# Three layer norms of a decoder layer: the turns of the last columns behind the second half's sums, vectors and residual columns loaded later

## The chip, the cores and the metric

The kernel runs on one core of a Trainium2 chip. TensorE (PE) multiplies and transposes into PSUM; VectorE (DVE) and ScalarE (ACT) work on SBUF and PSUM; SyncE (SP) issues nearly all DMAs; GpSimd (POOL) does little here. The metric is the time of one execution on the device in microseconds, the median of several. Each engine has one queue of instructions and runs it in the order in which the program wrote it; semaphores tie the engines together.

## The reference

A post-norm decoder layer on 256 tokens, 2048 wide, in float32. Cut to what matters here:

```
h = layer_norm(alpha*h + 0.5*swiglu(h, w_ffn1_gu, w_ffn1_down))          # norm 0
rq, rk, rv, rg, aq, ak, av, gate_r, gate_a = split(h @ w_in)
mixed = (sigmoid(gate_r)*ret_branch + sigmoid(gate_a)*att_branch) @ w_mix_out
h = layer_norm(alpha*h + mixed)                                          # norm 1
h = layer_norm(alpha*h + 0.5*swiglu(h, w_ffn2_gu, w_ffn2_down))          # norm 2
ple = sigmoid(h @ w_ple_gate) * (p @ w_ple_proj)
h = layer_norm(alpha*h + ple)                                            # norm 3
```

`layer_norm` takes mean and variance over the 2048 columns of a token, then `(x - mu)*rsqrt(var + eps)*g + b`. The change is at norms 0, 1 and 2 and at their borders with the next matrix product.

## The kernel before, in words

**Products.** Every float32 matrix is split into a high part (a copy rounded to the fast matmul type, on ACT, L91) and a low part (source minus high part, on DVE, L92); a product is three matmuls, low x high, high x high, high x low (L291 to L293). Activations stand transposed in a tile `ht`, `[128, 16, 512]`: index k is a group of 128 of the 2048 columns, and its 512 places are 256 tokens of the high part and 256 of the low part. Four k make a column block of 512 columns, so there are column blocks 0 to 3. The tokens are two halves t = 0 and t = 1 of 128 each.

**Weights.** Weights come in chunks of 512 KB (two k by 512 output columns; `Chunk`, L94). A chunk is loaded by SP (L105), made (ACT cast L91, DVE subtract L92) and used; the work tiles live in 46 equal slots (L34, L55). A planner, `fill` (L184), runs while the program is written: it makes loaded chunks as long as those that are ready amount to less than `ahead` microseconds of matmuls (a plain chunk counts 12, L129) and there are slots, and it makes none while `quiet` is set, unless a chunk is wanted at once. `done` (L213) gives a chunk's slots back and calls `fill`. What `fill` makes goes into the queues of ACT and DVE at that point.

**Ending a product with a norm.** The last steps of the product ahead of a norm are held out (`held_out`, L399): 4 chunks at norm 0 and norm 1, 6 at norm 2. All are multiplied for t = 0 first, then for t = 1, so that the norm of the first half of the tokens runs on DVE under the matmuls of the second half. In the first round each chunk takes its time off `ahead`, and `quiet` is set at its last two steps (L409 to L411). `columns(t, n)` adds a block of the product to the residual and takes its statistics; `normal(t)` (L509) does this for the last block, computes mean and 1/sigma by eleven small DVE instructions and normalizes block 0.

**Turns.** `turn(t, c)` (L519) normalizes column block c+1 on DVE, then transposes column block c on PE (four transposes, L486, into a PSUM tile `lnps`) and writes its high part to `ht` by ACT and its low part by DVE. The product after the norm begins with its front chunks (`first`, L565): 6 steps for t = 0, then the same 6 for t = 1. They read k = 0 to 11 (blocks 0 to 2) at norm 0 (`w_rv`) and norm 2 (`w_pg`), and k = 0 to 5 (blocks 0 and 1) at norm 1 (`f2_gu`, two output blocks to each k). Right behind them comes the chunk with k = 12, 13 at norms 0 and 2 (L945, L1278), so block 3; at norm 1 six chunks lie between the front and block 3.

**The order of events.** The nine events of a norm come in one fixed order: turns (0,0) to (0,3), `normal(1)` (the second sums), turns (1,0) to (1,3), and after the last of them `quiet(False)`. The tuples of numbers handed to `run` and `first` say after which step each is written; `follow` (L530) does it. In the second round of `first` a step n writes its matmuls, then `done` (with its `fill`), then the events of n:

```
            for j, (key, k0, n) in enumerate(steps):
                tokens_chunk(kept[j].chunk, k0, lhs, [sums[t][n] for t in range(2)], (1,))
                done(kept[j])
                self.follow(len(steps) + j + 1, times)
```

At norms 0 and 1 two small products with `p` (`put_by`, L607) lie between the held steps and the front.

**Loads for the norm.** In the last part of a feed-forward block (`before_unit`, L854; 20 units at norm 0, 19 at norm 2) the residual columns of blocks 2 and 3 are loaded at units 11 and 12, and `load_for_norm` (L594) at unit 13 loads gain and bias (`ln_vectors`, four DMAs of 512 KB on SP, L461) and `p`; `make_for_norm` splits `p` at the last unit. `others` (L806) tells the planner how many slots are taken by other things.

Of the kernel before, what the change touches and what calls it, by code (L numbers as in the profile page):

```python
# [30 lines left out]
FRONT = 6  # L31
# [17 lines left out]
def layer(ctx: ExitStack, tc: tile.TileContext, io):  # L49
# [170 lines left out]
    def quiet(on):  # L220
        room["quiet"] = on
# [272 lines left out]
    class Norm:  # L494
# [32 lines left out]
            else:  # L527
                ln_turn(*args, 4 * c, 4, self.keep.get(c))

        def follow(self, n, times):  # L530


            while times and times[0] == n:
                times.pop(0)
                at, self.at = self.at, self.at + 1
                if at == 4:
                    self.normal(1)
                else:
                    self.turn(at // 5, at % 5)
                if at == 8:  # L540
                    quiet(False)

        def run(self, steps, lhs, times, blks=()):


            self.vectors = vectors.pop()
            self.new = big.tile([P, KD, 512], F32R, tag="ht", name=f"ht{self.i}")
            per = len(steps) // len(self.cols)
            self.at, times = 0, list(times)

            def of_columns(t, j):
                if (j + 1) % per == 0 and j + 1 < len(steps):
                    self.columns(t, j // per)

            held_out(steps, lhs, self.sums, of_columns, lambda: self.normal(0), lambda n: self.follow(n, times))
            if blks:
                put_by(blks, lambda n: self.follow(2 * len(steps) + n, times))
            assert not times

        def put_away(self):  # L560
            if self.away is not None:
                for c in range(4):
                    sync.dma_start(self.away[c], self.y[c])

        def first(self, steps, lhs, sums, times):  # L565


            kept, times = [], list(times)
            for j, (key, k0, n) in enumerate(steps):
                u = take(key)  # L570
                kept.append(u)
                tokens_chunk(u.chunk, k0, lhs, [sums[t][n] for t in range(2)], (0,))
                fill()
                self.follow(j + 1, times)
            for j, (key, k0, n) in enumerate(steps):
                tokens_chunk(kept[j].chunk, k0, lhs, [sums[t][n] for t in range(2)], (1,))
                done(kept[j])
                self.follow(len(steps) + j + 1, times)
            assert self.at == 9
            self.put_away()  # L580

    def block_stats(stats, y, col):
# [3 lines left out]
    def load_columns(src, col, name):  # L586
        v = slot([P, 2, 512], F32, f"{name}{col}")
        sync.dma_start(v, src[col])
        return v
# [1 line left out]
    pp = {}  # L591
    p_raws, p_parts, vectors = [], [], []

    def load_for_norm(i):  # L594

        vectors.append(ln_vectors(i))
        if i < 2:
            p_raws.append(slot([P, 2, S], F32, "praw"))
            sync.dma_start(p_raws[0], io["pT"])
# [114 lines left out]
    def down_keys(name, b):  # L714
        return lambda n, p: (name + "_down", 2 * b + n, p)
# [9 lines left out]
    def ffn(name, i, ht, norm, keep, residual, keepers, away):  # L725
# [28 lines left out]
        for j in range(KF // 4):  # L754
            pg, pu = banks(f"{name}g{j}"), banks(f"{name}u{j}")
            units = gu_units(j)
            plain = len(units) - sum(kind == "S" for kind, p in units)
            n_of = {(0, 0): KD, (0, 1): KD, (1, 0): KD, (1, 1): KD}
            for kind, p in units:
                if kind == "S":  # L760
                    for at in ((0, 0), (0, 1), (1, 0)):
                        n_of[at] -= 1
                    n_of[1, 1] -= 2
            sums = [[Sum((pg, pu)[n][t], n_of[t, n]) for n in range(2)] for t in range(2)]
            got = []

            if norm is not None and j == 0:
                front, units = units[:FRONT_PAIRS], units[FRONT_PAIRS:]
                steps = [(gu_keys(name, 0)(n, p), 2 * p, n) for _, p in front for n in range(2)]
                norm.first(steps, rhs, sums, (4, 6, 7, 8))  # L770
                slots_for_weights(24)

            def before(u, j=j, offset=KD // 2 - len(units)):
                u += offset
                if j == 0 and norm is None and u % 2 == 0:
                    first_chunk(u // 2)
                    if u == 6:
                        slots_for_weights(24)
                    if u == 2:
                        load_constants()  # L780
                        lazy.append(rotary_tables())
                if j == 0 and u == 7:
                    for g in sorted({p // 2 for p in SEVEN}):
                        hi, lo = (slot([P, 8, P], F32R, f"{name}f{w}{g}") for w in "hl")
                        made[g] = seven_forms(keep[g], hi, lo)
                if j == KF // 4 - 1 and u in (4, 6):
                    convert(u // 2 - 2)

            block(f"{name}{j}", units, gu_keys(name, j), rhs, forms, sums, lambda *a: got.extend(seven_common(*a)), before)
            if got:  # L790
                g, v = got
                for x, ps in ((g, pg), (v, pu)):
                    for t in range(2):
                        dve.tensor_tensor(x[:, t], x[:, t], ps[t], ALU.add)  # L794
                act.activation(g, g, AF.Silu)  # L795
                dve.tensor_tensor(v, g, v, ALU.mult)
            else:
                v = slot([P, 2, 512], F32, f"{name}v{j}")
                for t in range(2):
                    act.activation(v[:, t], pg[t], AF.Silu)  # L800
                for t in range(2):
                    dve.tensor_tensor(v[:, t], v[:, t], pu[t], ALU.mult)
            later(2, lambda j=j, v=v: turned(j, v))
        stats = small.tile([P, 2, 4, 6], F32, tag="stats", name=name + "st", bufs=1)

        def others(n, ahead=45):  # L806

            slots_for_weights(SLOTS - 4 - n, ahead, max(90, ahead + 12))
# [43 lines left out]
            last[p // 2] = at  # L852

        def before_unit(u):  # L854
            others(2 * sum(at >= u for at in last.values()) + (4 if u < 12 else 9), 45 if u < len(second) - 5 else last_ahead)
            if u in (11, 12):
                y[u - 9] = load_columns(residual, u - 9, name + "y")
            if u == 13:
                load_for_norm(i)
            if u == len(second) - 1:  # L860
                make_for_norm()

        pt_ = [banks(f"{name}e{t}") for t in range(2)]
        sums = [[Sum(pt_[t][n], n_of[1][t, n]) for n in range(2)] for t in range(2)]
        block(f"{name}d1", second, down_keys(name, 1), lhs, forms, sums, fold(1), before_unit)
        slots_for_weights(27, last_ahead, last_ahead + 24)
        steps = [(down_keys(name, 1)(n, p), 2 * p, n) for n in range(2) for p in held]

# [1 line left out]
            dve.tensor_tensor(sl, sl, p, ALU.add)  # L870

        norm = Norm((2, 3), sums, combine, y, stats, i, 4 * LN_EPS, keepers, away)
        norm.run(steps, lhs, *(((8, 10, 11, 12, 12), (0, 1)) if i < 2 else ((8, 11),)))
        return norm


# [45 lines left out]
    def mixers(ht, norm, residual, keepers, away):  # L922
# [17 lines left out]

        ps = banks("rv0")
        sums = [[Sum(ps[t], KD)] for t in range(2)]
        norm.first([(("w_rv", 0, c), 2 * c, 0) for c in range(FRONT)], rhs, sums, (4, 6, 7, 8))
        slots_for_weights(24)
        for c in range(FRONT, KD // 2):  # L945
            u = take(("w_rv", 0, c))
# [275 lines left out]
        slots_for_weights(16)  # L1222
        for blk in range(3):
            if blk == 2:
                load_for_norm(1)
            ps = banks(f"mo{blk}")
            y[blk] = load_columns(residual, blk, "mixy")
            tokens_out(("w_mix", blk), KD, lhs, ps)
            for t in range(2):
                dve.scalar_tensor_tensor(y[blk][:, t], y[blk][:, t], ALPHA, ps[t], ALU.mult, ALU.add)  # L1230
            block_stats(stats, y, blk)
# [10 lines left out]
            run_side()  # L1242
        steps = [(("w_mix", 3, c), 2 * c, 0) for c in range(first, KD // 2)]
        norm = Norm((3,), sums, combine, y, stats, 1, LN_EPS, keepers, away)
        norm.run(steps, lhs, (8, 10, 11, 12, 12), (2, 3))
        return norm


    def embedding(ht, norm, y):
# [17 lines left out]
        for blk in range(4):  # L1267
# [4 lines left out]
            if blk == 0:  # L1272
                for j in range(4):
                    pp[j] = load_columns(pp, j, "ppr")
                steps = [(key + (c,), 2 * c, 0) for c in range(FRONT)]
                norm.first(steps, lhs, [[s] for s in sums], (1, 3, 3, 6, 7, 9, 10))
                slots_for_weights(24)
                for c in range(FRONT, KD // 2):  # L1278
                    u = take(key + (c,))
                    tokens_chunk(u.chunk, 2 * c, lhs, sums, (0, 1))  # L1280
                    done(u)
            elif blk < 3:
                for c in range(KD // 2):
                    u = take(key + (c,))
                    tokens_chunk(u.chunk, 2 * c, lhs, sums, (0, 1))
                    done(u)
                    run_side()
# [162 lines left out]
```

## Time and profile before

| what | value |
|---|---|
| median of 3 runs | 2315.0 us (2314.92 to 2315.1) |
| the profiled execution | 2312.8 us, of which the span is 2311.0 us |
| PE, DVE, ACT busy | 99%, 81%, 50% of the span |
| granted TensorE clock, mean | 0.996 |
| the chain that ended last | 95% PE, 3% DVE, 1% issue |
| norm 0, held steps to block 3's first use | about 695 to 738 us |
| norm 1 | about 1480 to 1519 us |
| norm 2 | about 2182 to 2226 us |

Matmuls are pipelined and their ends are modelled in the records: a matmul of 512 columns is shown as 0.39 us, yet the next one starts 0.227 us later (705.64, 705.87, 706.10 us). A wait of PE is therefore read from the distance of two starts, less 0.23 us, and is a little longer than the idle time in the list of waits. Times of a row are from the start of the span.

### The profile page before, as it was taken

How to read it: one execution, taken by the hardware profiler on the slowest of the kernel's cores; microseconds unless marked ns; L12 is line 12 of the kernel's file. 1: busy time of each engine (PE TensorE's matmuls, PEld its weight loads, DVE VectorE, ACT ScalarE, POOL GpSimd, SP SyncE). 2: the span in 40 equal slices, each digit the busy share in tenths (PEclk: the TensorE clock that was granted, in tenths of full speed). 3: DMA queues.
4: the chain of work that ended last, by engine and by line, in shares of the span. 5: the costliest groups of instructions: out<-in, count | busy, mean ns of one | idle time of the engine just before them, and what ended most of it. 6: DMA issues, size and time to landing. Idle time of an engine off the chain costs nothing.

```text
span 2311.0 us, 28634 instructions
## 1 busy us (share of the span) xinstructions
PE 2279.6 (99%) x10502; PEld 1887.7 (82%) x10502; DVE 1871.4 (81%) x2348; ACT 1162.9 (50%) x1404; POOL 97.0 (4%) x53
## 2 busy tenths in 40 slices
PE   9999999999999999999999999999999999999997
PEld 7788888888887888888778888888888888888876
DVE  7999999988988874677655555779999999889876
ACT  5555555565553342434554543355565555655432
POOL 0000000000000530133000000000000000000000
PEclk9999999999999999999999999999999999999999
DMA  9566666665587565546556667476666566565771
GB/s 316 164 218 191 194 208 194 197 218 182 201 287 263 176 225 160 170 150 198 159 158 183 184 207 260 161 249 207 192 191 212 182 204 217 172 219 193 289 255 55
DMA packets 193725, 465.70 MB, mean 202 GB/s; under 512 B 14768, under 2 KB 16048, under 8 KB 193584
## 3 DMA queue, kind: packets, MB, share of 16 engines
q1 hardware_dynamic: 191456, 460.91, 60.7%
q10 hardware_dynamic: 2128, 2.97, 0.4%
q8 instruction: 82, 1.34, 0.2%
q14 instruction: 59, 0.48, 0.1%
HBM read 455.43 MB, written 8.39 MB: 201 GB/s over the span
## 4 chain that ended last, share of the span: by engine, by line
PE 95%; DVE 3%; issue 1%; DMA 0%; ACT 0%; DVEq 0%; ACTq 0%
PE f2g L293 3%; PE f2g L291 3%; PE f2g L292 3%; PE f1g L291 3%; PE gt L291 3%; PE f1g L292 3%; PE f1g L293 3%; PE rqk L242 3%; PE gt L292 3%; PE gt L293 3%; PE f2u L291 2%; PE f2u L292 2%; PE f2u L293 2%; PE f1u L292 2%; PE f1u L291 2%; PE f1u L293 2%
## 5 line engine op out<-in xcount | busy, mean ns | idle before, releaser
L92 DVE TENSOR_TENSOR lf_gu<-rf_gu,hf_gu 128x1024 fp32r<-128x1024 f32 (+1 forms) x283 | 334.5, 1215 | 10.1 <-ACT hf_gu L91 9.7
L91 ACT CAST hf_gu<-rf_gu 128x1024 fp32r<-128x1024 f32 (+1 forms) x283 | 282.0, 1046 | 19.1 <-DMA rf_gu<-in_f_gu 18.8
L92 DVE TENSOR_TENSOR lw_in_f<-rw_in_f,hw_in_f 128x1024 fp32r<-128x1024 f32 x148 | 208.2, 1439 | 61.7 <-ACT hw_in_f L91 59.1
L92 DVE TENSOR_TENSOR lf_down<-rf_down,hf_down 128x1024 fp32r<-128x1024 f32 x152 | 180.9, 1221 | 28.2 <-ACT hf_down L91 23.2
L91 ACT CAST hf_down<-rf_down 128x1024 fp32r<-128x1024 f32 x152 | 155.5, 1051 | 77.7 <-DMA rf_down<-in_f_down 24.4
L91 ACT CAST huf_gu<-uf_gu 128x1024 fp32r<-128x1024 f32 x70 | 73.8, 1054 | 158.9 <-DVE uf_gu L164 153.2
L91 ACT CAST hw_in_f<-rw_in_f 128x1024 fp32r<-128x1024 f32 x148 | 145.8, 1051 | 0.2
L291 PE MATMUL f1g<-hf_gu,xt 128*128 128x512 f32 x247 | 97.3, 394 | 5.3 <-ACT hf_gu L91 5.3
L291 PE MATMUL gt<-hw_in_f,ht 128*128 128x512 f32 x256 | 102.5, 400 | 0.0
L292 PE MATMUL gt<-hw_in_f,ht 128*128 128x512 f32 x256 | 99.9, 390 | 0.0
L293 PE MATMUL gt<-lw_in_f,ht 128*128 128x512 f32 x256 | 99.9, 390 | 0.0
L292 PE MATMUL f1g<-hf_gu,xt 128*128 128x512 f32 x247 | 96.9, 392 | 0.0
L293 PE MATMUL f1g<-lf_gu,xt 128*128 128x512 f32 x247 | 96.8, 392 | 0.0
L291 PE MATMUL f2g<-hf_gu,ht 128*128 128x512 f32 x247 | 96.5, 391 | 0.0
L293 PE MATMUL f2g<-lf_gu,ht 128*128 128x512 f32 x247 | 96.2, 389 | 0.0
L292 PE MATMUL f2g<-hf_gu,ht 128*128 128x512 f32 x247 | 96.1, 389 | 0.0
L91 ACT CAST hvf_gu<-vf_gu 128x1024 fp32r<-128x1024 f32 x70 | 73.8, 1055 | 29.7 <-DVE vf_gu L166 29.7
L92 DVE TENSOR_TENSOR luf_gu<-uf_gu,huf_gu 128x1024 fp32r<-128x1024 f32 x70 | 85.3, 1219 | 0.0
L92 DVE TENSOR_TENSOR lvf_gu<-vf_gu,hvf_gu 128x1024 fp32r<-128x1024 f32 x70 | 85.3, 1218 | 0.0
L795 ACT ACTIVATE eve<-eve 128x1024 f32<-128x1024 f32 x20 | 21.2, 1062 | 127.0 <-DVE eve L794 127.0
L291 PE MATMUL f2u<-hf_gu,ht 128*128 128x512 f32 x212 | 83.5, 394 | 0.0
L291 PE MATMUL f1u<-hf_gu,xt 128*128 128x512 f32 x212 | 83.3, 393 | 0.0
(1053 smaller groups left out, 6275.1 us busy)
## 6 DMA issues: line engine op xcount, KB each, us to landing
rf_gu<-in_f_gu SPq DMA_DIRECT2D x351, 512.0 KB, 5.0
rf_down<-in_f_down SPq DMA_DIRECT2D x176, 512.0 KB, 4.5
rw_in_f<-in_w_in_f SPq DMA_DIRECT2D x148, 512.0 KB, 4.1
rw_rv<-in_w_rv SPq DMA_DIRECT2D x32, 512.0 KB, 4.4
rw_ret<-in_w_ret SPq DMA_DIRECT2D x32, 512.0 KB, 4.2
rw_mix<-in_w_mix SPq DMA_DIRECT2D x32, 512.0 KB, 4.5
rw_pg<-in_w_pg SPq DMA_DIRECT2D x32, 512.0 KB, 4.8
rw_att<-in_w_att SPq DMA_DIRECT2D x16, 512.0 KB, 4.1
```

The source lines that it names most:

```text
L91: act.copy(dst_hi, src)
L92: (lo_engine or dve).tensor_tensor(dst_lo, src, dst_hi, ALU.subtract)
L242: pe.matmul(ps[f], hi[:, kk, f * P : (f + 1) * P], rhs(k), start=k == 0, stop=k == n_k - 1,)
L291: pe.matmul(o, al, bh, start=first, stop=False)
L292: pe.matmul(o, ah, bh, start=False, stop=False)
L293: pe.matmul(o, ah, bl, start=False, stop=self.left == 0)
L795: act.activation(g, g, AF.Silu)
```

## The change

Each norm now has its own list of events, pairs of a step and either a turn, "sums" (`normal(1)`) or "go" (`quiet(False)`).

- Norm 0: turns (0,0), (0,1), (0,2) after steps 8, 10, 11 as before; sums after 11 in place of 12. In the front: (1,0) after 4, (1,1) after 6, (1,2) after 8 (was 7), go after 8, then (0,3) after 10 and (1,3) after 11 (were 12 of the part before, and 8).
- Norm 1: (0,0) after 8, (0,1) after 10, sums after 10 (was 12). In the front: (1,0) after 3, (1,1) after 5, (0,2) after 7, (1,2) and go after 8, (0,3) after 9, (1,3) after 10.
- Norm 2: (0,0) and (0,1) as before; (0,2) after step 1 of the front as before, and sums after 1 (was 3); (1,0), (1,1), (1,2) after 6, 7, 9 as before, go after 9 (was 10), (0,3) after 10 (was 3), (1,3) after 11 (was 10).
- Loads at norms 0 and 2, where n is the number of units: residual columns at units n-6 and n-5, `p` at n-3, gain and bias at n-1, just ahead of the last unit; `p` is split after the block. The slot numbers told to the planner follow. At norm 1 `p` is loaded ahead of gain and bias, at the same place.

```diff
-            while times and times[0] == n:
-                times.pop(0)
-                at, self.at = self.at, self.at + 1
-                if at == 4:
+            while events and events[0][0] == n:
+                what = events.pop(0)[1]
+                if what == "sums":
                     self.normal(1)
+                elif what == "go":
+                    quiet(False)
                 else:
-                    self.turn(at // 5, at % 5)
-                if at == 8:
-                    quiet(False)
+                    self.turned.append(what)
+                    self.turn(*what)
...
-    def load_for_norm(i):
-
-        vectors.append(ln_vectors(i))
+    def load_p(i):
+
         if i < 2:
...
-                norm.first(steps, rhs, sums, (4, 6, 7, 8))
+                norm.first(steps, rhs, sums, (
+                    (3, (1, 0)), (5, (1, 1)), (7, (0, 2)), (8, (1, 2)), (8, "go"), (9, (0, 3)), (10, (1, 3)),
+                ))
...
-            others(2 * sum(at >= u for at in last.values()) + (4 if u < 12 else 9), 45 if u < len(second) - 5 else last_ahead)
-            if u in (11, 12):
-                y[u - 9] = load_columns(residual, u - 9, name + "y")
-            if u == 13:
-                load_for_norm(i)
-            if u == len(second) - 1:
-                make_for_norm()
+            n = len(second)
+            held = 4 + 2 * (u >= n - 5) + (u >= n - 3) + 4 * (u >= n - 1)
+            others(2 * sum(at >= u for at in last.values()) + held, 45 if u < n - 5 else last_ahead)
+            if u in (n - 6, n - 5):
+                y[u - n + 8] = load_columns(residual, u - n + 8, name + "y")
+            if u == n - 3:
+                load_p(i)
+            if u == n - 1:
+                vectors.append(ln_vectors(i))
...
         block(f"{name}d1", second, down_keys(name, 1), lhs, forms, sums, fold(1), before_unit)
+        make_for_norm()
...
-        norm.run(steps, lhs, *(((8, 10, 11, 12, 12), (0, 1)) if i < 2 else ((8, 11),)))
+        if i < 2:
+            norm.run(steps, lhs, ((8, (0, 0)), (10, (0, 1)), (11, (0, 2)), (11, "sums")), (0, 1))
+        else:
+            norm.run(steps, lhs, ((8, (0, 0)), (11, (0, 1))))
...
-        norm.first([(("w_rv", 0, c), 2 * c, 0) for c in range(FRONT)], rhs, sums, (4, 6, 7, 8))
+        norm.first([(("w_rv", 0, c), 2 * c, 0) for c in range(FRONT)], rhs, sums, (
+            (4, (1, 0)), (6, (1, 1)), (8, (1, 2)), (8, "go"), (10, (0, 3)), (11, (1, 3)),
+        ))
...
-                load_for_norm(1)
+                load_p(1)
+                vectors.append(ln_vectors(1))
...
-        norm.run(steps, lhs, (8, 10, 11, 12, 12), (2, 3))
+        norm.run(steps, lhs, ((8, (0, 0)), (10, (0, 1)), (10, "sums")), (2, 3))
...
-                norm.first(steps, lhs, [[s] for s in sums], (1, 3, 3, 6, 7, 9, 10))
+                norm.first(steps, lhs, [[s] for s in sums], (
+                    (1, (0, 2)), (1, "sums"), (6, (1, 0)), (7, (1, 1)), (9, (1, 2)), (9, "go"),
+                    (10, (0, 3)), (11, (1, 3)),
+                ))
```

More of the change, by code (lines that the diff above doesn't have):

```diff
@@ L528, in turn, with follow, run @@
                 ln_turn(*args, 4 * c, 4, self.keep.get(c))
-        def follow(self, n, times):
-            while times and times[0] == n:
-                times.pop(0)
-                at, self.at = self.at, self.at + 1
-                if at == 4:
+        def follow(self, n, events):
+            while events and events[0][0] == n:
+                what = events.pop(0)[1]
+                if what == "sums":
                     self.normal(1)
-                else:
-                    self.turn(at // 5, at % 5)
-                if at == 8:
-                    quiet(False)
-        def run(self, steps, lhs, times, blks=()):
+                elif what == "go":
+                    quiet(False)
+                else:
+                    self.turned.append(what)
+                    self.turn(*what)
+        def run(self, steps, lhs, events, blks=()):
             self.vectors = vectors.pop()
@@ L548, in run @@
             per = len(steps) // len(self.cols)
-            self.at, times = 0, list(times)
+            self.turned, events = [], list(events)
             def of_columns(t, j):
@@ L553, in of_columns @@
                     self.columns(t, j // per)
-            held_out(steps, lhs, self.sums, of_columns, lambda: self.normal(0), lambda n: self.follow(n, times))
+            held_out(steps, lhs, self.sums, of_columns, lambda: self.normal(0), lambda n: self.follow(n, events))
             if blks:
-                put_by(blks, lambda n: self.follow(2 * len(steps) + n, times))
-            assert not times
+                put_by(blks, lambda n: self.follow(2 * len(steps) + n, events))
+            assert not events
         def put_away(self):
@@ L563, in put_away, with first @@
                     sync.dma_start(self.away[c], self.y[c])
-        def first(self, steps, lhs, sums, times):
-            kept, times = [], list(times)
+        def first(self, steps, lhs, sums, events):
+            kept, events = [], list(events)
             for j, (key, k0, n) in enumerate(steps):
@@ L573, in first @@
                 fill()
-                self.follow(j + 1, times)
+                self.follow(j + 1, events)
             for j, (key, k0, n) in enumerate(steps):
@@ L577, in first @@
                 done(kept[j])
-                self.follow(len(steps) + j + 1, times)
-            assert self.at == 9
+                self.follow(len(steps) + j + 1, events)
+            assert not events and len(set(self.turned)) == 8
             self.put_away()
```

## The prediction

> **What bounds the kernel now.** The page comes first: PE is busy for 99% of the span and the chain that ended last is 95% PE, so only what makes PE wait, or run slower, can move the time. Then PE's waits, whose first three rows add to 7.6 us of 2311 and lie at the norms. Then the clock: PE runs at half rate in two stretches behind such waits.
>
> ```profile
> PE 2279.6 (99%) x10502; PEld 1887.7 (82%) x10502; DVE 1871.4 (81%) x2348; ACT 1162.9 (50%) x1404; POOL 97.0 (4%) x53
> ...
> PE lnps L486 <- DVE f1y L479: 3.5, 3, 2.8
> PE lnps L486 <- DVE f2y L479: 2.8, 4, 1.6
> PE pg L291 <- DVE ht L92: 1.3, 1, 1.3
> PE lnps L486 <- DVE mixy L479: 1.2, 3, 0.5
> ...
> 709.70:713.10 3.40, 3.00 (x8) 2.47 (x9) 3.33 (x7) 0.74 (x2) 0.00 (x0) 0.50 0.02 10
> 2215.00:2218.40 3.40, 3.40 (x12) 2.72 (x11) 1.28 (x3) 0.59 (x1) 0.00 (x0) 0.50 0.78 230
> ```
>
> In the last two rows 0.50 is the granted clock. Last I read the order of the queues in time. At norm 0 the last high and low parts of `ht` are those of turn (1,3); right behind them ACT and DVE work through eight weight chunks without a gap:
>
> ```profile
> 732.81 0.59 ACT L91 CAST ht<-lnps 128x512 fp32r<-128x512 f32 x1 [1.25 <-PE lnps L486]
> 733.30 2.00 ACT L91 CAST hw_rv<-rw_rv 128x1024 fp32r<-128x1024 f32 x2
> 735.20 5.79 ACT L91 CAST hw_in_f<-rw_in_f 128x1024 fp32r<-128x1024 f32 x6
> ...
> 731.82 0.69 DVE L92 TENSOR_TENSOR ht<-lnps,ht 128x512 fp32r<-128x512 f32 x1
> 733.43 0.69 DVE L92 TENSOR_TENSOR ht<-lnps,ht 128x512 fp32r<-128x512 f32 x1 [0.93 <-ACT ht L91]
> 734.38 2.36 DVE L92 TENSOR_TENSOR lw_rv<-rw_rv,hw_rv 128x1024 fp32r<-128x1024 f32 x2 [0.25 <-ACT hw_rv L91]
> 736.66 6.90 DVE L92 TENSOR_TENSOR lw_in_f<-rw_in_f,hw_in_f 128x1024 fp32r<-128x1024 f32 x6
> ```
>
> At norm 2 the second sums' chain starts only behind turn (0,3)'s low part, and PE stands for it three times:
>
> ```profile
> 2206.43 0.69 DVE L92 TENSOR_TENSOR ht<-lnps,ht 128x512 fp32r<-128x512 f32 x1 [2.33 <-ACT ht L91]
> 2207.03 0.68 DVE L870 TENSOR_TENSOR f2y<-f2y,f2e 128x512 f32<-128x512 f32 x1
> ...
> 2211.49 0.44 PE L486 MATMUL lnps<-ident,f2y 128*128 128x128 f32 x2 [1.60 <-DVE f2y L479]
> 2212.49 0.41 PE L486 MATMUL lnps<-ident,f2y 128*128 128x128 f32 x2 [0.57 <-DVE f2y L479]
> 2214.18 0.50 PE L291 MATMUL pg<-hw_pg,ht 128*128 128x512 f32 x1 [1.28 <-DVE ht L92]
> ```
>
> **The sums earlier (gains).** No work is added or dropped; PE, DVE and ACT run the same instructions in another order.
> Norm 0: the second sums no longer stand behind turn (0,3). They began at 720.03 us and can begin when (0,2)'s low part is done (718.4): 1.6 us earlier. Turn (1,0) was ready at 724.57 and, for its second pair, at 725.49, where PE had 0.51 and 0.67 us of waits by the distance of starts. PE also arrives 0.4 us earlier, without (0,3)'s transposes. Both waits go: -1.2 us.
> Norm 1: the waits by starts are 0.50, 0.47, 0.67 and 0.54 us, 2.2 together. The sums start behind (0,1)'s low part (1496.8, was 1500.2); turn (1,0) comes one step sooner and its second pair waits about 0.6 us. -1.6 us. Here block 3 is first read six chunks (16.3 us) after the front, so the late turns (0,3) and (1,3) cost nothing; without that cover they would cost what follows.
> Norm 2: the sums start at 2204.0 instead of 2207.03, 3.0 us earlier; PE arrives about 2209.1, so the waits of 1.76 and 0.73 us (by starts) shrink to 0.2: -2.3. The third, 1.3, stays: it is the next normalization on DVE ahead of the low part. With 1.3 us of waiting instead of 3.9 the half-rate stretch behind it should go; its matmuls lie 0.43 us apart for 0.227, an excess of 1.6 us in all. -1.6.
>
> **Turns (0,3) and (1,3) behind "go" (the loss).** At norm 0 "go" is given after step 8. Step 9 calls `done`, so `fill` runs; the turns come at 10 and 11. How much `fill` makes: `ahead` is 136 less 4 x 12 = 88, a chunk counts 12, so it makes until eight are ready. All eight go into ACT's and DVE's queues ahead of turn (0,3). Before, they stood behind turn (1,3) (the rows above: 2 and 6). PE needs block 3 of t = 0 right behind the front. With 0 at the start of the front's second round: PE has six steps of six matmuls (6 x 0.227 = 1.36 us) and three turns at 0.47, and wants block 3 at 9.6 us. ACT ends (1,2)'s cast about 4.0, DVE its low part about 5.0; eight subtractions at 1.14 us (6.90 / 6 and 2.36 / 2) last to 14.2, then (0,3)'s low part 0.7: 14.9. PE waits 5.3 us. ACT's eight casts at 0.95 are done by 11.7 and are not the last.
> At norm 2, `ahead` is 136 - 6 x 12 = 64, so six chunks; "go" at 9, `fill` at 10, ahead of (0,3). From the start of (1,2)'s transposes PE wants block 3 after 5.5 us (three steps, three turns); DVE ends (1,2)'s low part at 1.95 (2220.49 to 2222.44), six subtractions from 2.2 last to 9.1, plus 0.7: 9.8. PE waits 4.3 us. (1,3)'s low part follows within PE's next step in both places.
> Bounds: nothing (if those chunks stood elsewhere) to 6.5 and 5.5 us (ACT's queue one cast later). I take the worked values, as all durations are rows of these very instructions.
> Each of the two waits should bring the half rate once. The row: 1.3 to 1.6 us of excess a stretch; I take 1.5 each, from 0 to 3 (two stretches). That is +3.0.
> The Trainium skill, "TensorE: Matmul & The Clock Gate", section "Why this matters for your kernels", advises to leave no idle gap of PE over about 3 us, as that halves the clock. The row of 2215 us differs: none of the gaps before it is over 1.8 us. By the rule the new waits would halve the clock just the same, but the stretch at 2215 would not hang on the waits that go, and the sum would be 1.6 us higher.
>
> **Vectors at the last unit.** Norm 0: four DMAs of 512 KB are now written between the loads of `w_rv` chunks 4 and 5. SP had issued these at 695.41 and 695.83, each as a slot came free; they landed 1.27 us apart, chunk 5 at 700.27. The four slots that gain and bias held are free until then, so chunk 4 can go at about 692.7; the vectors follow at 693.0 to 696.0 as slots come free and chunk 5 at 696.4, landing fifth in line at 702.6, 2.3 us later. Its cast (1.05), its subtraction (1.23) and the split of `p` (0.69, now behind it) stand ahead of the first half's statistics on DVE, which began at 703.42 and would at 705.5. Turn (0,0), for which PE already stands 2.9 us, comes 2.1 us later: +2.1. Bounds: -2.4 (the freed slots end the wait of the last `w_rv` subtraction, and the statistics begin with the last matmul of t = 0 at 701.0) to +5.1 (4 x 1.27). I take the worked one, the nearest to SP's rows.
> Norm 2: the same order, but DVE was late there by its own work; chunk 5 lands about 1 us later and the statistics move by 0.5: +0.5 (-0.5 to +1.5). The residual columns land within 10 us, 10 us or more ahead of their use: nothing. Norm 1: same place, nothing.
>
> **Sum.** Norm 0: 2.1 - 1.2 + 5.3 + 1.5 = +7.7. Norm 1: -1.6. Norm 2: -2.3 - 1.6 + 0.5 + 4.3 + 1.5 = +2.4. Together +8.5 us. The profiled execution took 2312.8, so 2321.3; the median of the runs, 2315.0, is 2.2 above it, so **2323.5 us**, 0.37% slower.
>
> **Rivals.**
> (a) Not slower: the chunks made at "go" do not stand ahead of the last turns. If only the two that block 3 itself needs were made, the waits would be 5.3 - 6 x 1.14 and 4.3 - 4 x 1.14, so none, and without their half rates the sum is 8.5 - 12.6 = -4.1: 2310.9. It decides from about three chunks down. For it: `fill` also asks for slots. Against: at the same step before it made all eight and all six.
> (b) The order holds, but the clock does not fall and the vector loads are hidden: 8.5 - 3.0 - 2.1 = +3.4, 2318.4. For it: half rate is granted in fixed steps (the stretches begin 441 x 3.413 us apart), so a wait may be shared between two. Against: 2.5 us of standing within one step was enough at 2215.
> (c) Worse: all four vector loads lie in the way (+5.1) and each new wait brings two stretches: 8.5 + 3.0 + 3.0, 2329.5. For it: PE already stands at that place; against: SP's freed slots.
> (d) The half rate at 2215 stays though the waits before it shrink: +1.6, 2325.1. For it stands the skill's rule above; against it the row itself, which follows 3.9 us of broken standing.
>
> **How the numbers follow.** Forecast 0.60, (a) 0.10, (b) 0.14, (c) 0.11, (d) 0.05. 0.2% is 4.6 us, about what this kernel's measurement can tell from no change. Slower: the forecast, (c), (d) and a little of (b), 0.78; same: the rest of (b) and half of (a), 0.17; faster: 0.05, (a) with the vector loads hidden (-6.2). The range leaves out (a), some of (c) and the ends of (b): 2316 to 2328.5.
>
> **What would show it.** Right: a wait of PE of 4 to 6 us at `rv` L291 or L292 near 740 us, released by DVE `ht` L92, and one of 3.5 to 5 at `pg` near 2220; in DVE's order eight and six weight subtractions ahead of two last `ht`; no wait at turn (1,0) of norms 0 and 2; the wait at turn (0,0) of norm 0 about 5 instead of 2.8. Wrong: the two last `ht` ahead of the chunks, or no wait at block 3.

## The result and the profile after

| | before | after |
|---|---|---|
| median | 2315.0 us (2314.92 to 2315.1) | 2327.5 us (2326.3 to 2329.88) |
| profiled execution / span | 2312.8 / 2311.0 us | 2327.4 / 2325.6 us |

The ratio is 1.0057 (95% interval 1.0041 to 1.0073); by the medians the change costs 12.5 us. A second set of both kernels, below, gives 1.0061 (1.0047 to 1.0074) and 14.2 us.

The busy time of the engines, from the page of the changed kernel:

```profile
PE 2282.6 (98%) x10502; PEld 1889.8 (81%) x10502; DVE 1870.0 (80%) x2348; ACT 1161.7 (50%) x1404; POOL 96.9 (4%) x53
```

And PE's waits in its trace (total, times, longest, in us):

```profile
PE lnps L486 <- DVE f1y L479: 7.5, 2, 7.3
PE pg L291 <- DVE ht L92: 5.4, 2, 4.1
...
PE rv L291 <- DVE ht L92: 5.0, 1, 5.0
PE lnps L486 <- DVE f2y L479: 3.0, 3, 2.3
...
PE lnps L486 <- DVE mixy L479: 0.3, 1, 0.3
```

The count of matmuls is the same; PE's share fell by a point. Two rows are as forecast: `rv` 5.0 and the 4.1 inside `pg` are the new waits for block 3 (1.3 of `pg` was there before). The first row, 7.3 in one wait, was forecast as about 5. The row of `f2y` is no smaller than before (2.8), though the waits at turn (1,0) are gone: a new one of 2.3 at turn (0,0) took their place. `mixy` fell from 1.2 to 0.3.

The block-3 waits are read from DVE's order in time (start, duration, last column the idle time before and its releaser), first at norm 0, then at norm 2:

```profile
736.48 0.69 DVE L92 TENSOR_TENSOR ht<-lnps,ht 128x512 fp32r<-128x512 f32 x1 [1.03 <-ACT ht L91]
737.43 2.36 DVE L92 TENSOR_TENSOR lw_rv<-rw_rv,hw_rv 128x1024 fp32r<-128x1024 f32 x2 [0.26 <-ACT hw_rv L91]
739.71 6.89 DVE L92 TENSOR_TENSOR lw_in_f<-rw_in_f,hw_in_f 128x1024 fp32r<-128x1024 f32 x6
746.52 1.28 DVE L92 TENSOR_TENSOR ht<-lnps,ht 128x512 fp32r<-128x512 f32 x2
...
2231.09 6.90 DVE L92 TENSOR_TENSOR lw_pg<-rw_pg,hw_pg 128x1024 fp32r<-128x1024 f32 x6 [0.25 <-ACT hw_pg L91]
2237.91 1.28 DVE L92 TENSOR_TENSOR ht<-lnps,ht 128x512 fp32r<-128x512 f32 x2
```

Eight and six weight subtractions now stand ahead of the two last `ht`, those of turns (0,3) and (1,3).

The first waits are read from SP, ACT and DVE of the same kernel ahead of the first half's statistics (L874 opens them), at norm 0 and then at norm 2:

```profile
692.95 2.40 SPq L461 DMA_DIRECT2D ln_g<-in_ln_g  x2
695.46 0.85 SPq L461 DMA_DIRECT2D ln_b<-in_ln_b  x2
696.40 7.34 SPq L105 DMA_DIRECT2D rw_rv<-in_w_rv  x3
...
704.99 1.05 ACT L91 CAST hw_rv<-rw_rv 128x1024 fp32r<-128x1024 f32 x1 [5.42 <-DMA rw_rv<-in_w_rv]
...
706.07 1.23 DVE L92 TENSOR_TENSOR lw_rv<-rw_rv,hw_rv 128x1024 fp32r<-128x1024 f32 x1 [5.25 <-ACT hw_rv L91]
707.21 0.68 DVE L92 TENSOR_TENSOR pt<-praw,pt 128x512 fp32r<-128x512 f32 x1
707.82 0.68 DVE L874 TENSOR_TENSOR f1y<-f1y,f1e 128x512 f32<-128x512 f32 x1
...
2200.47 1.05 ACT L91 CAST hw_pg<-rw_pg 128x1024 fp32r<-128x1024 f32 x1 [6.34 <-DMA rw_pg<-in_w_pg]
...
2201.56 1.22 DVE L92 TENSOR_TENSOR lw_pg<-rw_pg,hw_pg 128x1024 fp32r<-128x1024 f32 x1 [4.24 <-ACT hw_pg L91]
```

The chunks of the front are counted from 0, so chunk 5 is its sixth and last. The issues fall where the prediction put them (692.95 to 696.40). Chunk 5 lands at 704.91, not at 702.6; DVE does nothing for 5.25 us and the statistics begin at 707.82 (703.42 before, 705.5 forecast). At norm 2 DVE stands idle at the same place for 4.24 us.

The windows of the stretches at half rate (length, busy time of PE, PEld, DVE, ACT, POOL, then the granted clock, the DMA share and GB/s):

```profile
708.90:719.10 10.20, 5.25 (x14) 4.03 (x15) 9.67 (x24) 0.75 (x2) 0.00 (x0) 0.50 0.06 26
746.50:753.20 6.70, 5.95 (x14) 4.68 (x15) 1.30 (x3) 0.00 (x0) 0.00 (x0) 0.50 0.83 333
2238.10:2241.40 3.30, 2.75 (x7) 2.17 (x8) 1.09 (x2) 0.00 (x0) 0.00 (x0) 0.50 0.39 145
```

Before there were two stretches of 3.4 us at the norms; the one at 2215 is gone, as forecast.

### The profile page after: what moved, and what is told of

Read it like the earlier page. It is cut to its first block, busy times and chain, and to the rows that moved or that the text cites. A ratio compares the mean times of both kernels' runs of the same rounds, so it can differ in the third digit from the quotient of the medians.

```text
span 2325.6 us, 28634 instructions
## 1 busy us (share of the span) xinstructions
PE 2282.6 (98%) x10502; PEld 1889.8 (81%) x10502; DVE 1870.0 (80%) x2348; ACT 1161.7 (50%) x1404; POOL 96.9 (4%) x53
## 3 DMA queue, kind: packets, MB, share of 16 engines
q10 hardware_dynamic: 2128, 2.97, 0.4%
## 4 chain that ended last, share of the span: by engine, by line
PE 93%; DVE 4%; DMA 1%; issue 1%; ACT 1%; SPq 0%; ACTq 0%; DVEq 0%
PE f2g L293 3%; PE f2g L291 3%; PE f2g L292 3%; PE gt L291 3%; PE rqk L242 3%; PE gt L292 3%; PE gt L293 3%; PE f1g L291 2%; PE f1g L292 2%; PE f2u L291 2%; PE f2u L292 2%; PE f2u L293 2%; PE f1g L293 2%; PE f1u L292 2%; PE f1u L291 2%; PE f1u L293 2%
```

## The experiments

**The theory.** Three things make the time: (1) chunks made at "go" ahead of turns (0,3) and (1,3); (2) the vector loads, which put off the landing of chunk 5, for which DVE stands ahead of the statistics; (3) the second sums earlier, a gain of 6.7 us. **The rivals**: that the new order itself lengthens the first waits and the loads are hidden; that the long first wait belongs to one execution; that the late turns' work only comes back at the next place.

Each run is compared with the kernel before on the same chip (its medians there were 2314.1 to 2314.4 us):

| run | median us | ratio, 95% interval | first wait, norm 0 / 2 | wait at block 3, norm 0 / 2 |
|---|---|---|---|---|
| before, again | 2313.1 (one run) | - | 2.97 / 0.0 | - |
| loads alone | 2322.0 | 1.0036 (1.0024 to 1.0049) | 8.12 / 2.22 | - |
| order alone | 2322.0 | 1.0036 (1.0023 to 1.0049) | 4.87 / 0.0 | 5.20 / 4.28 |
| after, turns first | 2313.6 | 0.9997 (0.9989 to 1.0006) | 7.33 / 2.54 | - |
| sums alone | 2307.3 | 0.9970 (0.9958 to 0.9982) | 4.91 / 0.2 | - |
| sums, two chunks late | 2305.8 | 0.9964 (0.9951 to 0.9976) | 0.0 / 0.0 | - |
| the same, new loads | 2305.5 | 0.9962 (0.9949 to 0.9974) | 0.0 / 0.0 | - |
| fewer chunks at "go" | 2319.1 | 1.0018 (1.0009 to 1.0027) | 6.82 / 2.65 | 2.92 / 0.88 |
| vectors behind chunk 6 | 2319.8 | 1.0024 (1.0015 to 1.0033) | 3.24 / 0.0 | 5.16 / 4.28 |
| one chunk late, behind (0,0) | 2302.8 | 0.9951 (0.9938 to 0.9963) | 0.0 / 0.0 | - |
| one chunk late, behind (0,1) | 2304.2 | 0.9957 (0.9944 to 0.9969) | 0.0 / 0.0 | - |
| after, again | 2328.3 | 1.0061 (1.0047 to 1.0074) | 6.80 / 2.77 | 5.16 / 4.27 |

Waits here are distances of two starts of PE less the usual pitch, in us. "First wait" is that for the first pair of transposes of turn (0,0).

### Loads alone, order alone, and the sums without the losses

The first run is the kernel before with the loads of the changed one:

```diff
-            others(2 * sum(at >= u for at in last.values()) + (4 if u < 12 else 9), 45 if u < len(second) - 5 else last_ahead)
...
+            held = 4 + 2 * (u >= n - 5) + (u >= n - 3) + 4 * (u >= n - 1)
...
+            if u == n - 1:
+                vectors.append(ln_vectors(i))
```

> The order of events of before, the loads of after (gain, bias, p and residual columns nearer to use, slot numbers with them). Theory, that the traces add up: the growth of the first wait at norm 0 (2.9 to 7.5 us) and at norm 2 (0.1 to 2.5 us) comes from the vector loads alone, so both waits show here, and some 1.5 us of half rate behind the longer one: 4.5 + 2.4 + 1.5 = 8.4, 2323.4 us. Rival, the prediction's own sizes (2.1 + 0.5): 2317.6 us, which would mean that the late landings of after's trace belong to that one execution. Rival, that the new order lengthens these first waits and the loads are hidden: 2315 us, first waits as before.

The second is the changed kernel with all edits of the loads undone.

> The order of events of after, the loads of before. Theory: the first waits are 2.9 and 0.1 us as before; turn (1,0) waits no more; block 3 is waited for 5.2 and 4.3 us, each with its half rate: 12.5 for the whole change less 8.4 for the loads = 4.1, 2319.1 us. The prediction's sizes give 2315 + 5.9 = 2320.9 us. Rival, that the order lengthens the first waits: first waits of 7 and 2.4 us here too, 2327 us.

The third is the changed kernel with the late turns written ahead of "go":

```diff
-            (4, (1, 0)), (6, (1, 1)), (8, (1, 2)), (8, "go"), (10, (0, 3)), (11, (1, 3)),
+            (4, (1, 0)), (6, (1, 1)), (8, (1, 2)), (8, (0, 3)), (8, (1, 3)), (8, "go"),
...
-                    (1, (0, 2)), (1, "sums"), (6, (1, 0)), (7, (1, 1)), (9, (1, 2)), (9, "go"),
-                    (10, (0, 3)), (11, (1, 3)),
+                    (1, (0, 2)), (1, "sums"), (6, (1, 0)), (7, (1, 1)), (9, (1, 2)), (9, (0, 3)),
+                    (9, (1, 3)), (9, "go"),
```

> After, with turns (0,3) and (1,3) of norms 0 and 2 written ahead of go (norm 0: all at step 8; norm 2: all at step 9). Theory: the eight and six weight chunks now stand behind the two turns, so the waits of 5.2 and 4.3 us at block 3 go, with 0 to 3 us of half rate: 2327.5 - 9.5 - 1.5 = 2316.5 us. Rival, that the same DVE work is only late at the next place (the chunks that block 3 meets, or the turns that now come three in a row): a wait of 3 us or more in the 15 us behind the front of each norm, 2321 us or more.

The fourth is both edits at once: the turns ahead of "go" and the loads of before.

> The second sums earlier as in after, turns (0,3) and (1,3) behind them but ahead of go, the loads of before: the gains of the change without its two losses. Theory: -1.2 at norm 0, -1.6 at norm 1, -2.3 and -1.6 (half rate) at norm 2, together -6.7: 2308.3 us. Rival, that DVE is the limit of the whole stretch and the time comes back as a wait at the later turns or at block 3: 2313 to 2316 us, with new waits there.

Loads alone cost 7.9 us (8.4 expected) and show the long first waits. ACT's and DVE's rows of that run, in time:

```profile
705.73 1.05 ACT L91 CAST hw_rv<-rw_rv 128x1024 fp32r<-128x1024 f32 x1 [7.28 <-DMA rw_rv<-in_w_rv]
...
706.81 1.23 DVE L92 TENSOR_TENSOR lw_rv<-rw_rv,hw_rv 128x1024 fp32r<-128x1024 f32 x1 [7.10 <-ACT hw_rv L91]
```

So the rival "the order lengthens the first waits" falls, and so do the prediction's sizes for this term (2.6 us).

Order alone also costs 7.9 us, more than the 4.1 and 5.9 expected. Its waits at block 3 are the expected ones; 1.9 us of the surplus is a longer first wait (4.87 for 2.94), because chunk 5 landed 7.2 us after its issue in this trace (4.4 in the trace before). The new order did not cause that: in both traces PE, DVE, ACT and SP run the same instructions in the same order until 718 us, and the chunk lands at 702.7. The two parts make 15.8 us and the whole change 12.5 to 14.2, so they do not add up exactly; the late landing in order alone accounts for some of it, and the rest is inside the intervals (each about 3 us either way).

With the turns ahead of "go" both block-3 waits go and 13.7 us with them (2327.3 by the ratio of the changed kernel, 2313.6 here, 2316.5 expected). DVE's rows at norm 0 of that run:

```profile
736.20 1.89 DVE L92 TENSOR_TENSOR ht<-lnps,ht 128x512 fp32r<-128x512 f32 x3 [1.07 <-ACT ht L91]
738.12 2.36 DVE L92 TENSOR_TENSOR lw_rv<-rw_rv,hw_rv 128x1024 fp32r<-128x1024 f32 x2
740.40 5.76 DVE L92 TENSOR_TENSOR lw_in_f<-rw_in_f,hw_in_f 128x1024 fp32r<-128x1024 f32 x5
```

Three `ht` in a row, then the chunks, and no new wait behind the front: the rival "late at the next place" falls. Without the loads as well, the gain is 6.8 us, where 6.7 was expected: the earlier sums were worth what the prediction said, to within the interval, and the kernel that has them alone is 0.30% faster than the one before.

### How many chunks stand ahead of block 3

An integer in the list of events sets `ahead` and takes the place of "go".

```diff
-            (4, (1, 0)), (6, (1, 1)), (8, (1, 2)), (8, "go"), (10, (0, 3)), (11, (1, 3)),
+            (4, (1, 0)), (6, (1, 1)), (8, (1, 2)), (8, 72), (10, (0, 3)), (11, (1, 3)),
...
-                    (1, (0, 2)), (1, "sums"), (6, (1, 0)), (7, (1, 1)), (9, (1, 2)), (9, "go"),
+                    (1, (0, 2)), (1, "sums"), (6, (1, 0)), (7, (1, 1)), (9, (1, 2)), (9, 36),
...
+                elif isinstance(what, int):
+                    quiet(False)
+                    room["ahead"] = what
```

> After, but at go only six chunks are made at norm 0 (eight in after) and three at norm 2 (six in after) ahead of turn (0,3). Theory: each chunk is worth 1.14 us of the wait at block 3: 5.2 - 2 x 1.14 = 2.9 us at norm 0, 4.3 - 3 x 1.14 = 0.9 us at norm 2; with 1 to 3 us of half rate less, 2327.4 - 5.7 - 2 = 2319.7 us. Rival, that the wait hangs on ACT or on the transposes and not on the count of chunks: waits of 5.2 and 4.3 us as in after, 2327 us.

Measured 2319.1 us, 2319.7 expected. DVE's order at both norms:

```profile
736.61 2.36 DVE L92 TENSOR_TENSOR lw_rv<-rw_rv,hw_rv 128x1024 fp32r<-128x1024 f32 x2 [0.26 <-ACT hw_rv L91]
738.89 4.62 DVE L92 TENSOR_TENSOR lw_in_f<-rw_in_f,hw_in_f 128x1024 fp32r<-128x1024 f32 x4
743.43 1.28 DVE L92 TENSOR_TENSOR ht<-lnps,ht 128x512 fp32r<-128x512 f32 x2
...
2227.95 3.50 DVE L92 TENSOR_TENSOR lw_pg<-rw_pg,hw_pg 128x1024 fp32r<-128x1024 f32 x3 [0.26 <-DMA ln_b<-in_ln_b]
2231.36 1.28 DVE L92 TENSOR_TENSOR ht<-lnps,ht 128x512 fp32r<-128x512 f32 x2
```

The waits are 2.92 and 0.88 us for 2.9 and 0.9 expected. Each chunk fewer takes one subtraction (1.14 us) off PE's wait, and the rival, ACT or the transposes, falls. From these sizes one would estimate that the wait is gone at three chunks at norm 0 and at two at norm 2; no run tried it.

### Vectors behind chunk 6

```diff
-            if u == n - 1:
-                vectors.append(ln_vectors(i))
...
         block(f"{name}d1", second, down_keys(name, 1), lhs, forms, sums, fold(1), before_unit)
+        vectors.append(ln_vectors(i))
         make_for_norm()
```

> After, with the four vector loads of norms 0 and 2 written behind the block instead of ahead of its last unit, so that chunks 5 and 6 of the front are loaded ahead of them. Theory (place in line): chunk 5 lands as without them, the first waits fall to those of the run with the new order and the old loads (about 4.5 and 0.1 us): 2327.4 - 5.4 = 2322 us. Rival (slots or the pull on the chip's memory, whatever the place in line): first waits of 7.5 and 2.5 us as in after, 2327 us. A third way is that the vectors now land behind the statistics and the first normalization waits for them: a first wait of more than 7.5 us, 2329 us or more.

2319.8 us (2322 expected): the first waits fall to 3.24 and 0, and the third way is out. ACT's row for chunk 5 and SP's rows behind it:

```profile
700.26 1.05 ACT L91 CAST hw_rv<-rw_rv 128x1024 fp32r<-128x1024 f32 x1 [2.60 <-DMA rw_rv<-in_w_rv]
...
695.89 0.86 SPq L461 DMA_DIRECT2D ln_g<-in_ln_g  x2
696.84 5.28 SPq L461 DMA_DIRECT2D ln_b<-in_ln_b  x2
```

The vectors are as late as in the changed kernel, or later; only their place in line differs. Chunk 5 was issued at 694.99, 1.4 us sooner than in the changed kernel, and landed at 700.16, 4.7 us sooner. It is the place in line that costs.

### The last chunks made behind the statistics

If DVE stands for chunk 5 ahead of the statistics, it need not: the front wants that chunk some 20 us later. The planner's reach is lowered so that only four of the front's chunks are made ahead of the norm, and two are made behind turn (0,0). The reach of the loads stays as it was.

```diff
-        last_ahead = 136
+        last_ahead = 112
...
+                elif what == "two":
+                    quiet(False)
+                    room["ahead"] += 24
+                    fill()
+                    quiet(True)
...
-            norm.run(steps, lhs, ((8, (0, 0)), (10, (0, 1)), (11, (0, 2)), (11, "sums")), (0, 1))
+            norm.run(steps, lhs, ((8, (0, 0)), (8, "two"), (10, (0, 1)), (11, (0, 2)), (11, "sums")), (0, 1))
```

Norm 2 has the same event behind its turn (0,0). Once with the loads of before:

> The order of the run with the sums earlier and the loads of before, and besides: of the front's six weight chunks only four are made ahead of the norm, the last two right behind turn (0,0), at norms 0 and 2. Theory: the first wait at norm 0 is DVE standing for the landing of the last chunk that is made ahead of the first half's statistics; without it the statistics begin when PE ends t = 0 (701.1 instead of 705.5), and the wait of 4.9 us falls to about 0.6, with up to 1.5 us of half rate: 2307.3 - 4.3 - 1 = 2302 us (2300.5 to 2303.5). Rival, that DVE's two subtractions (2.4 us) only move the lateness behind turn (0,0): waits of 2 to 4 us at turns (0,1) to (1,0) or at the fifth chunk, 2306 to 2309 us.

And once with those of the changed kernel:

> The same late making of two chunks, with the loads of after. Theory: the vector loads cost time only because they delay the chunk that DVE waits for ahead of the statistics; with that chunk out of the way they cost nothing, so the time is that of the run with the loads of before, within 1 us: about 2302 us, first waits at norms 0 and 2 of 0.6 us each. Rival, that the vectors themselves land too late for the first normalization, or that the slots they take delay the weights: 6 us above that run, as between the two runs without late making.

2305.8 and 2305.5 us, where about 2302 was expected of both. The two sets of loads differed by 6.2 us ahead of this edit (2313.6 and 2307.3) and by nothing behind it: what the loads cost, they cost through the chunk that DVE waits for. One thing is mixed in: with fewer slots in use the vectors were issued 3 us sooner (from 689.85), so the second run alone does not tell an earlier issue from a wait that is gone.

With the loads of before, the 4.9 us of first wait are gone, yet the gain is only 1.5 us: the rival's wait came in their place. DVE's rows of the run with new loads:

```profile
709.63 2.35 DVE L92 TENSOR_TENSOR lw_rv<-rw_rv,hw_rv 128x1024 fp32r<-128x1024 f32 x2
711.89 0.75 DVE L478 SCALAR_TENSOR_TENSOR f1y<-f1y,mv,ln_g 128x512 f32<-128x512 f32 x1
712.68 0.75 DVE L479 SCALAR_TENSOR_TENSOR f1y<-f1y,rstd,ln_b 128x512 f32<-128x512 f32 x1
```

The two late subtractions stand ahead of the normalization for turn (0,2), and PE waits there for 2.2 us at norm 0 and 1.8 at norm 2. Hence two runs that make only one chunk late:

```diff
-        last_ahead = 112
+        last_ahead = 124
...
+                elif what == "one":
+                    quiet(False)
+                    was, room["ahead"] = room["ahead"], sum(u.time for u in ready) + 1
+                    fill()
+                    room["ahead"] = was + 12
+                    quiet(True)
```

Behind turn (0,0):

> As the run with late making and the loads of after, but only the sixth weight chunk of the front is made late (behind turn (0,0)); the fifth is made ahead of the norm again. Theory: the wait of 2.2 and 1.8 us at turn (0,2) was the two subtractions of 1.2 us ahead of its normalization on DVE; with one of them it is 1.0 and 0.6 us, and the fifth chunk lands in time: 2305.5 - 2.4 = 2303 us. Rival, that DVE now stands for the fifth chunk: a wait of 1 to 3 us at turn (0,0) in place of it, 2305 to 2307 us.

Behind turn (0,1):

> The same with the sixth chunk made behind turn (0,1). Theory: its subtraction now stands behind the normalization for turn (0,2), which waits no more, but ahead of the second sums, which begin 0.5 to 1 us later: a wait of up to 1 us at turn (1,0): 2302.5 us. Rival, that the second sums are late by the whole 1.2 us at both norms and PE waits as much as with the chunk behind (0,0): 2303 to 2304 us.

2302.8 us, 0.49% faster than before, where 2303 was expected; behind (0,1) 2304.2, where 2302.5 was expected. There PE waits 0.9 and 0.7 us for the two pairs of transposes of turn (1,0) at norm 0 and 0.3 and 0.6 us at norm 2, where a stretch at half rate comes with it; that is nearer to the rival. The windows around norms 0 and 2 of the better one:

```profile
700.00:740.00 40.00, 38.79 (x187) 31.80 (x186) 36.55 (x67) 17.35 (x26) 0.00 (x0) 1.00 0.77 291
2183.00:2225.00 42.00, 39.77 (x188) 31.83 (x187) 36.95 (x67) 17.67 (x25) 0.00 (x0) 1.00 0.81 298
```

PE is at full clock through both. Its five runs lie within 0.7 us (2302.58 to 2303.27), those of before on the same chip within 3.6 (2312.91 to 2316.5).

### Both kernels again

> The kernel before once more, for its trace: on the chip of these runs. Theory: where the half-MB loads land varies from execution to execution by 2 to 3 us; chunk 5 of the front lands 4.4 to 6.5 us after it is issued (4.4 in the trace shown, 6.4 to 7.2 in the two runs with the same loads), and the first wait at norm 0 is 2.9 to 5 us. Rival, that the earlier landing belongs to the kernel before: 4.4 us and 2.9 us again.

> The changed kernel once more, on the chip of these runs, for a second trace and a narrower ratio. Theory: waits at block 3 of 5.2 and 4.3 us as before, to 0.1 us, since they are made of instructions' lengths alone; first waits of 6.5 to 8 us at norm 0 and 2.2 to 2.7 at norm 2, since these hang on landings; 2327 us. Rival, that the long first wait belongs to the one execution profiled: 4 to 5 us.

The waits at block 3 return to within 0.02 us, and the long first waits return with the changed kernel (6.80 and 2.77), so they belong to the kernel. For the kernel before, chunk 5 landed 5.3 us after its issue (4.4 in the first trace) and the first wait was 2.97: the landing is on the theory's side, and the wait fits both. In two runs with the same loads but the new order of events (order alone, sums alone) it took 7.2, though PE, DVE, ACT and SP had run the same instructions in the same order as in the kernel before. So the order is not the cause, and the landing of the same work differs by 2.8 us from trace to trace. Whether the chip has a part in it is open: those two ran on one chip, the second trace of the kernel before on another.

## Why the prediction was right, and where it was off

2323.5 us was forecast, 2316 to 2328.5, slower; 2327.5 was measured. Direction and mechanism were right; two terms were too small, the vector loads and the half rate. That the time lay inside the range is in part luck: the range ended 13.5 us above the kernel before, and the second set gives 14.2. Rival (c), 2329.5, which had both terms larger, came closer than the forecast. The terms, with the sizes from the two pairs of traces (a first wait is here that of both pairs of transposes of turn (0,0)):

| step | predicted | first pair | second pair |
|---|---|---|---|
| vector loads: first wait, norm 0 | +2.1 | +4.5 | +3.7 |
| vector loads: first wait, norm 2 | +0.5 | +2.4 | +2.8 |
| block 3, norm 0 | +5.3 | +5.2 | +5.2 |
| block 3, norm 2 | +4.3 | +4.3 | +4.3 |
| turn (1,0), norm 0 | -1.2 | -1.2 | -1.2 |
| turns of norm 1 | -1.6 | -1.7 | -1.7 |
| turn (1,0), norm 2 | -2.3 | -2.5 | -2.5 |
| matmuls at half rate, norm 0 | +1.5 | +3.4 | +2.6 |
| matmuls at half rate, norm 2 | -0.1 | 0.0 | +2.5 |
| sum | +8.5 | +14.4 | +15.7 |
| difference of the profiled executions | | +14.6 | +15.2 |

**The waits at block 3 and the gains** stood to 0.2 us a term, because they were sums of durations of these very instructions in an order that the program fixes. Rival (a), chunks that stand elsewhere, fell; the run with fewer chunks showed its scale (1.14 us each) to be right.

**The step that was mis-sized is the vector loads at the last unit.** The prediction took chunk 4's landing as 3.6 us after issue and five more landings at 1.27 us each, so 702.6. Issue was as forecast, but in five traces with these loads chunk 5 landed 7.8 to 9.1 us after it was issued (6.2 forecast): the line moves at 1.28 us a load for a while and stalls once or twice. In the profiled run of the changed kernel the stall came ahead of chunk 4, which landed 5.9 us after issue; in the run with the turns first the landings behind chunk 4 are 1.29, 2.04, 2.78, 1.29 and 1.27 us apart. The price of a load was read from a quiet stretch of the trace before, in which 140 of the 899 DMAs landed over 0.8 us later than that pace. The Trainium skill, "DMA: Bandwidth & Descriptors", section "Latency and other measured facts", gives 0.2 us for an access to the memory and 2 us at high load; the stalls above, 0.8 to 2.3 us, are of that size, and no run shows their cause.

At norm 2 the cover named in the prediction, DVE late by its own work, was gone: DVE stood 4.24 us for the chunk. It was issued 13.0 us ahead of PE's last matmul before turn (0,0), as in the trace before, but landed 7.5 us after issue and not 4.55, so 3 us later; the 1 us of the forecast had no row under it. At norm 0 the term came out between the forecast's +2.1 and the +5.1 of rival (c).

**The half rate** was forecast as one stretch of 1.5 us of excess for each new wait, and that was too small as well. Added up over the matmuls of each stretch, the waits at block 3 brought 1.3 to 2.8 us each, 2.3 on average, in the four traces that have them at full size (after, after again, order alone, vectors behind chunk 6); in seven of the eight places there were two stretches, as rival (c) had it. What was left out is that the longer first waits bring it too: 0.3 to 0.9 us more at norm 0, and at norm 2 a new stretch of 1.7 us in the second trace. Rival (d) fell: the stretch at 2215 went with the waits ahead of it, as the row of before had said. The 2.5 us of standing that the prediction counted there within one step were 2.2: the wait of 1.76 us ended at 2211.49, and the step began at 2211.55.

**Why the total came out closer than its terms**: the terms sum to 14.4 in the profiled pair, while the medians differ by 12.5. The profiled execution of before was 2.2 us below its median, as the prediction had noted, and that of after was at its own. That is luck; the sum itself was too small by 5.9.

## What to carry to other kernels

What a planner makes when a brake is released goes into the in-order queues at that point: whatever the next matrix product needs first has to be written ahead of the release, and once PE waits for it, each chunk ahead of it costs one subtraction (here 1.14 us) of PE's time. A transfer written ahead of a load that an engine waits for delays that load (with four of 512 KB moved behind it the first wait went from about 7 us to 3.2), so either put it behind in line or let the engine do the urgent chain first and convert the late chunk afterwards. And size a landing by the spread of landings in the trace, not by its fastest pace.

## What the runs showed of the hardware

The clock's steps can be told closely. All half-rate stretches begin on a grid of 3.413 us within their trace. Over the 14 traces, more than 9000 such steps at full rate were laid beside PE's standing time within each (waits of over 0.25 us by the distance of starts, less 0.23 us, or 0.11 behind a transpose; the stretch at the end of the kernel, behind the last matmul, is left out): all 29 steps with 2.04 us or more were followed by half rate, and none with 2.03 or less was. The line is good to about 0.1 us: with 0.23 taken off behind transposes too, a step of 1.92 halves the clock and one of 2.03 does not. It is the sum within a step that counts, not one gap: 0.3, 0.6 and 1.5 us that fell into one step halved the clock in the run with one chunk behind (0,1), while a lone wait of 1.8 us never did. From a half-rate step the clock came back when less than 1.1 us of standing fell in it, and stayed low from 1.18 on (45 steps). A wait of 4.28 us cost one stretch in one trace and two in the next, by where it fell on the grid. The Trainium skill, "TensorE: Matmul & The Clock Gate", section "What's actually happening", has the free-running window of about 3.4 us, and the trace agrees; it asks for a whole idle window, and here 60% of one was enough.
